# Layer 0's input projections: one 512-column product of the weights' high part with both parts of the input, in turns of 256 features

## The chip, the cores and the metric

The kernel runs on one core of a Trainium2 chip, as one launch. The metric is the time of the whole launch on the device, in microseconds. The times shown are the median of three runs; the profile comes from one more execution with the hardware profiler on.

## The reference

Two layers of a decoder trunk over 256 tokens of width 2048, in float32. Layer 0 is the one that the change touches:

```python
h = rms_norm(x, g_pre)
u = h @ w_in                      # (256 x 2048) @ (2048 x 8192)
xr, zr, xm, zm = jnp.split(u, [2048, 4096, 6144], axis=-1)
xr = causal_dwconv(xr, ...);  yr = rg_lru(xr, ...)
xmc = silu(causal_dwconv(xm, ...)); q, k = block_diag(xmc, ...); v = block_diag(xm, m_wv)
ym = head_norm(mlstm_chunkwise(q, k, v, ig, fg)) + m_skip * xmc
y = concat([yr * silu(zr), ym * silu(zm)])
x = x + rms_norm(y @ w_out, g_post)
```

Layer 1 is an RWKV-7 mixer with an input projection of 2048 x 16384 and an output projection of 4096 x 2048, with the same pre-norm, post-norm and residual.

## The kernel before, in words

**Number format.** The large products keep more precision than one pass of TensorE in fp32r gives. Each operand is split into a high part (a cast to fp32r) and a low part (the rest). A product is then the sum of three: weights high with input high, weights high with input low, weights low with input high. In the trace the parts of the weights are `whi` and `wlo`, the parts of the input `hh` and `hl`, those of the mixers' output `yh` and `yl`.

**Input projections.** `in_proj` (L242) makes 512 features of all 256 tokens. It takes eight weight tiles of 128 partitions x 1024 floats (two slabs of 128 input rows, 512 features each, 512 KB, one request of SyncE each in `load_w`, L216). `split_w` (L202) casts a tile on ScalarE (`whi`) and subtracts on VectorE (`wlo`). `in_mms` (L221) then issues 24 products: the weights are the stationary block (128 x 128), the input (features on partitions, 256 tokens) moves. Two PSUM banks (`gb`) hold the four blocks of 128 features. Layer 0 has 16 such projections, in three groups: four for `xm` (L680), four pairs for the LRU branch and its gate (L689), four for the mLSTM gate (L709). Layer 1 has 32 of the same form. There are four buffers for raw weights, three for `whi`, three for `wlo`.

**Output projections.** `out_proj` (L261) turns the roles round: the mixers' output is the stationary block, 512 columns of weights move, 768 products of 512 columns in each layer.

**The input.** `to_features` (L334) normalises the input and turns it so that features lie on partitions: a product with a diagonal matrix (`dg`), out of PSUM through ScalarE (`hh`) and VectorE (`hl`, L361 to L366). The first slab of 512 features is made ahead, the other three are made within the first projection, one when `in_proj` finds that it is needed soon (`next(grow[0])`).

**Order.** The order on TensorE is written out: `InOrder` (L102) chains its instructions. `Weave` interleaves the side work of the mixers (generators such as `mlstm_in`, `head`, `lru`) with the projections: `wv_.tick(dt)` moves a planned clock on, and each generator tells by `yield` when its next piece is due; `wv_.drain` issues what is left of one. The splits have a higher priority than other work of ScalarE and VectorE, and `Behind` (L123) keeps later rows behind them; the rest is ordered by the scheduler. Each engine runs its rows in that order. Because helpers issue everything, the trace shows all of TensorE's products at L117 or L120 and all of ScalarE's and VectorE's rows at L133; the names of the tiles tell them apart. `mb` are the PSUM banks of the side work.

**What takes a projection's result.** For `xm`, two ScalarE copies bring it to SBUF (`xm`), and `mlstm_in` of that block runs beside the next projection; its 80 products stand as one block behind that projection (`wv_.drain(prev)`). For the LRU branch, the convolution reads PSUM (`conv`, output `yc`); for the gates, `silu2` does.

Of the kernel before, what the change touches and what calls it, by code (L numbers as in the profile page):

```python
# [7 lines left out]
F32 = mybir.dt.float32  # L8
F32R = mybir.dt.float32r
# [4 lines left out]
P = 128  # L14
# [130 lines left out]
def two_layers(ctx, tc, x, gpost, cst, selc, v0, v1, w_in0, w_out0, w_in1, w_out1, lruw, qkvw,  # L145
# [9 lines left out]
    hp = ctx.enter_context(tc.tile_pool(name="hp", bufs=8))  # L155
# [3 lines left out]
    pg = ctx.enter_context(tc.tile_pool(name="pg", bufs=4, space=PS))  # L159
# [3 lines left out]
    def gbank():  # L163
        return pg.tile([P, 512], F32, name="gb", tag="gb")
# [56 lines left out]
    def in_mms(banks, hi, lo, pc, h, nft, tick):  # L221

        def mm(part, kk, f, hx, first=False, last=False):
            pe.matmul(banks[f // 2][:, (f % 2) * T:(f % 2 + 1) * T], lhsT=part[:, kk, f * P:(f + 1) * P], rhs=hx,
                      start=first, stop=last, skip_group_check=True)

        hs = [tuple(t[:, (2 * pc + kk) % 4, :] for t in h[(2 * pc + kk) // 4]) for kk in range(2)]
# [14 lines left out]
    def in_proj(wsrc, h):  # L242

        banks = [gbank(), gbank()]
# [7 lines left out]
    def half(banks, f):  # L252
        return banks[f // 2][:, (f % 2) * T:(f % 2 + 1) * T]

    def split_y(src, yl):
        yh = hp.tile([P, 4, T], F32R, name="yh", tag="hp")
# [4 lines left out]
    def out_proj(wsrc, get_y, evac, tick, finish, after, room=None):  # L261
# [22 lines left out]
        pair = [[gbank(), gbank()] for _ in range(2)]  # L284
# [9 lines left out]
        for c in range(2, 4):  # L294
            banks = [gbank(), gbank()]
# [38 lines left out]
    def to_features(xs, dg, g, warm):  # L334
# [14 lines left out]
        def tiles():  # L349
            banks[2] = [gbank(), gbank()]  # L350
# [5 lines left out]
            for c in range(4):  # L356
# [35 lines left out]
    def silu2(banks, sz):  # L392

        for b in range(2):
            bk = banks[b].rearrange("p (a t) -> p a t", a=2)
# [24 lines left out]
    with ExitStack() as l0:  # L420
# [257 lines left out]

        prev = None
# [9 lines left out]
        for c in range(4):  # L689
            lw = t4("lw")  # L690
            nc.sync.dma_start(lw.rearrange("p a t -> p (a t)"), lruw[:, c, :])
            banks = in_proj(w_in0[c * 8:(c + 1) * 8], h)
# [9 lines left out]
            banks = in_proj(w_in0[(4 + c) * 8:(5 + c) * 8], h)  # L702
# [6 lines left out]
        for c in range(4):  # L709
            banks = in_proj(w_in0[(12 + c) * 8:(13 + c) * 8], h)  # L710
# [31 lines left out]
    with ExitStack() as l1:  # L742
# [39 lines left out]
        def loras():  # L782

            banks = [gbank(), gbank()]
# [374 lines left out]
        for g in range(NG):  # L1159
            st = sts[g]  # L1160
            banks = in_proj(w_in1[(8 + g) * 8:(9 + g) * 8], h)
# [10 lines left out]
            banks = in_proj(w_in1[g * 8:(g + 1) * 8], h)  # L1172
# [4 lines left out]
            banks = in_proj(w_in1[(24 + g) * 8:(25 + g) * 8], h)  # L1177
# [7 lines left out]
            banks = in_proj(w_in1[(16 + g) * 8:(17 + g) * 8], h)  # L1185
# [116 lines left out]
```

## Time and profile before

| What | Value |
|---|---|
| Median of 3 runs | 1917.0 us (1916.63 to 1918.4) |
| The profiled execution's own time | 1918.1 us |
| Its span, first to last instruction | 1916.3 us |
| Granted TensorE clock, mean | 0.995 |
| TensorE busy | 1890.5 us, 16506 instructions |
| TensorE weight loads | 1753.2 us, 16507 instructions |
| VectorE busy | 1394.7 us |
| ScalarE busy | 1045.2 us |
| Transfers | 299.63 MB, mean 156 GB/s |
| Packets of the request queue | 86768, 45.0% of 16 engines' time |

A row of the chain or of the timeline gives the start in us from the span's start, the duration in us, the engine, and how many instructions were merged (x192). A group's row gives the line, the engine, the operation, output and inputs with their shapes, the count, busy time in us and the mean duration of one in ns; the durations of products overlap, so a pace is read from the chain and not from the mean. A row of the windows gives a stretch, its length, the busy time of TensorE, its weight loads, VectorE, ScalarE and GpSimd with instruction counts, the granted clock, the transfers' busy share and GB/s.

### The profile page before, as it was taken

To read this page: it belongs to the slowest core of one execution; us is meant where nothing else is said; L and a number is where in the kernel's file an instruction comes from. 1 tells how busy PE (TensorE), PEld (TensorE's weight loads), DVE (VectorE), ACT (ScalarE), POOL (GpSimd) and SP (SyncE) were. 2 spreads that over 40 slices of the span, in tenths; PEclk is the share of its full clock that TensorE was granted. 3 is DMA by queue.
4 is the path that set the end of the run, shared out by engine and by line. 5 is a ranking of instruction groups with operands and counts; after the bars stand their busy time and mean duration, and the time that the engine had idled before them with its cause. 6 is when DMAs were issued, how large, how long until landed. Compare 5 with 4: busy or idle time off the path is not lost.

```text
span 1916.3 us, 39538 instructions
## 1 busy us (share of the span) xinstructions
PE 1890.5 (99%) x16506; PEld 1753.2 (91%) x16507; DVE 1394.7 (73%) x2302; ACT 1045.2 (55%) x1609; POOL 59.1 (3%) x84
## 2 busy tenths in 40 slices
PE   9999999999999999999999999999999999999998
PEld 8999999999888899989999999999999999997886
DVE  5667777767555679879689689597796896895544
ACT  6445666645444546555565555655655655555442
POOL 0000000000000000000000000000000000000000
PEclk9999999999999999999999999999999999999999
DMA  7333544445666444423434334344343433356654
GB/s 254 138 133 111 176 165 171 152 173 197 214 202 202 165 144 147 155 106 137 143 130 143 123 130 157 109 150 146 116 147 133 141 133 133 122 186 201 211 202 156
DMA packets 86947, 299.63 MB, mean 156 GB/s; under 512 B 9576, under 2 KB 12392, under 8 KB 86768
## 3 DMA queue, kind: packets, MB, share of 16 engines
q1 hardware_dynamic: 86768, 297.11, 45.0%
q8 instruction: 129, 2.11, 0.4%
q14 instruction: 50, 0.41, 0.1%
HBM read 289.20 MB, written 7.86 MB: 155 GB/s over the span
## 4 chain that ended last, share of the span: by engine, by line
PE 93%; DVE 4%; ACT 1%; issue 1%; DMA 1%; POOL 0%; SPq 0%; DVEq 0%; POOLq 0%; ACTq 0%
PE gb L117 75%; PE mb L117 17%; DVE wlo L133 2%; PE mb L120 1%; ACT whi L133 1%; DVE wb L133 1%; DMA raw<-in_w_in_dram 0%; DVE rt L133 0%; DVE Tb L133 0%; DMA xq<-in_x_dram 0%; DVE tf L133 0%; DVE Ab L133 0%; DVE yT L133 0%; ACT ZT L133 0%; ACT vt L133 0%
## 5 line engine op out<-in xcount | busy, mean ns | idle before, releaser
L133 DVE TENSOR_TENSOR wlo<-raw,whi 128x1024 fp32r<-128x1024 f32 x509 | 619.6, 1218 | 344.2 <-ACT whi L133 308.4
L133 ACT CAST whi<-raw 128x1024 fp32r<-128x1024 f32 x509 | 532.3, 1048 | 553.4 <-PE gb L117 505.1
L117 PE MATMUL gb<-hh,whi 128*128 128x256 f32 x3120 | 793.5, 290 | 2.9 <-ACT whi L133 2.9
L117 PE MATMUL gb<-hl,whi 128*128 128x256 f32 x3120 | 773.7, 284 | 0.5 <-DVE hl L133 0.5
L117 PEld LDWEIGHTS gb<-hh,whi 128*128 128x128 f32 x3120 | 598.8, 192 | 13.6 <-ACT whi L133 3.7
L117 PEld LDWEIGHTS gb<-hl,whi 128*128 128x128 f32 x3120 | 600.0, 192 | 1.9 <-DVE hl L133 1.1
L117 PE MATMUL gb<-hh,wlo 128*128 128x256 f32 x3120 | 454.0, 286 | 0.0
L117 PEld LDWEIGHTS gb<-hh,wlo 128*128 128x128 f32 x3120 | 405.5, 192 | 4.2 <-issue 0.7
L117 PE MATMUL gb<-whi,yl 128*128 128x512 f32 x500 | 136.9, 392 | 0.5 <-DVE yl L133 0.5
L117 PE MATMUL gb<-whi,yh 128*128 128x512 f32 x500 | 136.5, 392 | 0.0
L117 PE MATMUL gb<-wlo,yh 128*128 128x512 f32 x500 | 135.7, 390 | 0.0
L117 PEld LDWEIGHTS gb<-whi,yl 128*128 128x128 f32 x500 | 93.2, 188 | 20.4 <-DVE yl L133 0.9
L117 PEld LDWEIGHTS gb<-wlo,yh 128*128 128x128 f32 x500 | 93.5, 188 | 19.7
L117 PEld LDWEIGHTS gb<-whi,yh 128*128 128x128 f32 x500 | 93.0, 188 | 19.3
L133 DVE TENSOR_TENSOR Tb<-Tb,tf 64x31 f32<-64x31 f32 (+15 forms) x248 | 82.5, 333 | 6.1
L133 DVE TENSOR_TENSOR tf<-Ab,Tb 64x31 f32<-64x31 f32 (+15 forms) x248 | 81.8, 330 | 4.5
L117 PE MATMUL mb<-AR,BK 64*128 64x128 f32 (+1 forms) x1024 | 58.0, 253 | 7.0 <-DVE AR L133 6.0
L117 PEld LDWEIGHTS mb<-AR,BK 64*128 64x128 f32 (+1 forms) x1024 | 50.2, 161 | 13.3 <-PE gb L117 7.1
L133 DVE TENSOR_TENSOR UV<-mb,Gn 64x256 f32<-64x256 f32 x64 | 26.9, 421 | 34.6 <-PE mb L117 33.4
L133 ACT ACTIVATE zz<-kP,dv 128x256 f32<-128x256 f32 x64 | 32.3, 505 | 22.9 <-DVE kP L133 12.4
L117 PEld LDWEIGHTS mb<-UV,At 128*64 128x64 f32 (+1 forms) x1024 | 35.0, 137 | 10.3 <-issue 2.2
L1140 POOL TENSOR_TENSOR vr<-vr,mhalf 128x8 f32<-128x8 f32 x16 | 28.3, 1771 | 505.5 <-DVE vr L133 505.5
(259 smaller groups left out, 1859.7 us busy)
## 6 DMA issues: line engine op xcount, KB each, us to landing
raw<-in_w_in_dram SPq DMA_DIRECT2D x384, 512.0 KB, 3.2
raw<-in_w_out_dram SPq DMA_DIRECT2D x128, 512.0 KB, 4.2
y1d<-zt SPq DMA_DIRECT2D x7, 512.0 KB, 3.5
yraw<-y1d SPq DMA_DIRECT2D x7, 512.0 KB, 3.8
l<-in_lora_dram SPq DMA_DIRECT2D x8, 384.0 KB, 4.3
xq<-in_x_dram SPq DMA_DIRECT2D x8, 256.0 KB, 4.4
lw<-in_lruw_dram SPq DMA_DIRECT2D x4, 512.0 KB, 4.9
xr<-in_x_dram SPq DMA_DIRECT2D x8, 256.0 KB, 6.3
```

Of the source, the lines that this page charges most:

```text
L117: return self._chain(self.eng.matmul(*a, **k))
L120: return self._chain(self.eng.transpose(**k))
L133: r = op(*a, **k)
L1140: pool.tensor_tensor(vr, vr, mhalf[:, 0:8], ALU.pow)
```

## The change

Layer 0's `in_proj` is rewritten; layer 1 keeps the old one under the name `in_proj1`. The high and low part of the input now lie beside each other in one tile `hx` (per slab row: 256 tokens of the high part, then 256 of the low), so that one product of 512 columns multiplies the weights' high part with both. A PSUM bank then holds one block of 128 features: the left half collects high with high, the right half high weights with the low input and low weights with the high input (products of 256 columns). As two banks hold only 256 features that way, a projection is done in two turns of 256 features, each over all 2048 input rows. A weight tile has 512 input rows of 256 features and comes by two requests with pieces of 256 floats. At a turn's end ScalarE copies the right half to an SBUF tile `u`, and VectorE adds the left half to it; what follows reads `u` instead of PSUM. The pools change to match: `hp` has four tiles of double size (`split_y` fills one in two steps), `pg` two pairs of banks. The planned clock moves on by 4 x 0.42 + 2 x 0.44 us for a tile of 16 products, where it was 6 x 0.44 for 24.

```diff
-    hp = ctx.enter_context(tc.tile_pool(name="hp", bufs=8))
+    hp = ctx.enter_context(tc.tile_pool(name="hp", bufs=4))
...
-    pg = ctx.enter_context(tc.tile_pool(name="pg", bufs=4, space=PS))
+    pg = ctx.enter_context(tc.tile_pool(name="pg", bufs=2, space=PS))
...
+    def gpair():
+        return pg.tile([P, 2, 512], F32, name="gb", tag="gb")
...
+    def in_proj(wsrc, h, mk):
+        u = None
+        for j in range(2):
+            t = gpair()
+            for pc in range(4):
+                raw = wp.tile([P, 2, 512], F32, name="raw", tag="raw", bufs=RAW_BUFS)
+                for n in range(2):
+                    src = wsrc[2 * pc + n].rearrange("p (k f) -> p k f", k=2)[:, :, j * 256:(j + 1) * 256]
+                    nc.sync.dma_start(raw[:, n].rearrange("p (k f) -> p k f", k=2), src)
+                hi, lo = (w.rearrange("p n (k f) -> p (n k) f", k=2) for w in split_w(raw))
+                if len(h) < 4 and len(h) <= pc + 1:
+                    next(grow[0])
+                for kk in range(4):
+                    for f in range(2):
+                        pe.matmul(t[:, f, :], lhsT=hi[:, kk, f * P:(f + 1) * P], rhs=h[pc][:, kk].rearrange("p a t -> p (a t)"),
+                                  start=(pc == 0 and kk == 0), stop=False, skip_group_check=True)
+                    wv_.tick(0.42)
+                for kk in range(4):
+                    for f in range(2):
+                        pe.matmul(t[:, f, T:2 * T], lhsT=lo[:, kk, f * P:(f + 1) * P], rhs=h[pc][:, kk, 0, :],
+                                  start=False, stop=(pc == 3 and kk == 3), skip_group_check=True)
+                    if kk % 2:
+                        wv_.tick(0.44)
+            if u is None:
+                u = mk()
+            act.copy(u[:, 2 * j:2 * j + 2, :], t[:, :, T:2 * T])
+            dve.tensor_tensor(u[:, 2 * j:2 * j + 2, :], t[:, :, 0:T], u[:, 2 * j:2 * j + 2, :], ADD)
+        return u
...
     def split_y(src, yl):
-        yh = hp.tile([P, 4, T], F32R, name="yh", tag="hp")
+        if not yhs:
+            pair = hp.tile([P, 2, 4, T], F32R, name="yh", tag="hp")
+            yhs.extend([pair[:, 1], pair[:, 0]])
+        yh = yhs.pop()
...
-                hh = hp.tile([P, 4, T], F32R, name="hh", tag="hp")
-                hl = hp.tile([P, 4, T], F32R, name="hl", tag="hp")
+                hx = hp.tile([P, 4, 2, T], F32R, name="hx", tag="hp")
                 for i in range(4):
                     bf = half(banks[c], i)
-                    activ(hh[:, i, :], bf, AF.Copy, scale=g(4 * c + i))
-                    dve.scalar_tensor_tensor(hl[:, i, :], bf, g(4 * c + i), hh[:, i, :].bitcast(F32), MUL, SUB)
-                h.append((hh, hl))
+                    activ(hx[:, i, 0, :], bf, AF.Copy, scale=g(4 * c + i))
+                    dve.scalar_tensor_tensor(hx[:, i, 1, :], bf, g(4 * c + i), hx[:, i, 0, :].bitcast(F32), MUL, SUB)
+                h.append(hx)
...
-            banks = in_proj(w_in0[(8 + c) * 8:(9 + c) * 8], h)
+            xm = in_proj(w_in0[(8 + c) * 8:(9 + c) * 8], h, u0)
             wv_.drain(prev)
-            xm = t4("xm")
-            for b in range(2):
-                act.copy(xm[:, 2 * b:2 * b + 2, :], banks[b].rearrange("p (a t) -> p a t", a=2))
             prev = wv_.add(mlstm_in(c, xm))
```

Three places show what moves. The first is TensorE at the start of layer 0's first projection; `dg` with `xq` are the turns of the input into feature order, four of a bank in a row. Before:

```order
L117 MATMUL mb<-dg,xq 128x128 x8
L117 MATMUL gb<-dg,xq 128x128 x4
L117 MATMUL mb<-dg,xq 128x128 x8
L117 MATMUL gb<-hh,whi 128x256
L117 MATMUL gb<-hl,whi 128x256
...
L117 MATMUL gb<-hh,wlo 128x256 x8
```

Now:

```order
L117 MATMUL gb<-hx,whi 128x512 x8
L117 MATMUL gb<-hx,wlo 128x256 x8
L117 MATMUL gb<-dg,xq 128x128 x4
L117 MATMUL gb<-hx,whi 128x512 x8
L117 MATMUL gb<-hx,wlo 128x256 x8
L117 MATMUL mb<-dg,xq 128x128 x8
L117 MATMUL gb<-hx,whi 128x512 x8
```

A weight tile has 16 products instead of 24, and the next turn of the input stands behind each of the first two tiles. In all, TensorE has 1024 products fewer; from the first output projection on its rows are the same as before.

The second place is VectorE at the same time, where the pieces of the input's slabs (`hx`, out of `gb` for the third slab) and the splits (`wlo`) share the engine. Now, from the second weight tile on:

```order
L133 SCALAR_TENSOR_TENSOR hx<-mb,vec_97,hx 128x256
L133 TENSOR_SCALAR lt<-vec_97 128x16
L133 TENSOR_TENSOR wlo<-raw,whi 128x1024
L133 SCALAR_TENSOR_TENSOR hx<-gb,vec_97,hx 128x256
L133 TENSOR_TENSOR wlo<-raw,whi 128x1024
L133 SCALAR_TENSOR_TENSOR hx<-gb,vec_97,hx 128x256
L133 TENSOR_TENSOR wlo<-raw,whi 128x1024
L133 SCALAR_TENSOR_TENSOR hx<-gb,vec_97,hx 128x256
L133 TENSOR_TENSOR lt<-vec_97,lt 128x16
L133 SCALAR_TENSOR_TENSOR hx<-mb,vec_97,hx 128x256
L133 TENSOR_SCALAR lt<-lt 128x16
L133 SCALAR_TENSOR_TENSOR hx<-mb,vec_97,hx 128x256
```

The row behind these is the third slab's last piece (`hx` out of `gb` again). Before, the rows of the constants' table (`lt`) and more splits stood between the slabs' pieces, which were spread over twice as many weight tiles.

The third place is VectorE at the end of the second `xm` projection, around the blocks of the mLSTM weights (`we`). Before:

```order
L133 SCALAR_TENSOR_TENSOR xm_792<-th,xc 128x1024
L133 TENSOR_TENSOR we<-qkvs,cs_112 128x128 x3
L133 TENSOR_TENSOR wlo<-raw,whi 128x1024
L133 TENSOR_TENSOR we<-qkvs,cs_112 128x128 x9
L133 TENSOR_TENSOR wlo<-raw,whi 128x1024
L133 TENSOR_TENSOR we<-qkvs,cs_112 128x128 x3
```

Now:

```order
L133 SCALAR_TENSOR_TENSOR xm_682<-th,xc 128x1024
L133 TENSOR_TENSOR we<-qkvs,cs_112 128x128 x3
L133 TENSOR_TENSOR wlo<-raw,whi 128x1024
L133 TENSOR_TENSOR we<-qkvs,cs_112 128x128 x8
L133 TENSOR_TENSOR wlo<-raw,whi 128x1024
L133 TENSOR_TENSOR u<-gb,u 128x512
L133 TENSOR_TENSOR we<-qkvs,cs_112 128x128 x4
```

The addition of the projection's second turn, which waits for its last product, stands ahead of the last four `we` blocks. In layer 1, VectorE and ScalarE keep their instructions, but some of them stand in another order than before.

More of the change, by code (lines that the diff above doesn't have):

```diff
@@ L158, in two_layers, with gbanks @@
     sp = ctx.enter_context(tc.tile_pool(name="small", bufs=2))
-    pg = ctx.enter_context(tc.tile_pool(name="pg", bufs=4, space=PS))
+    pg = ctx.enter_context(tc.tile_pool(name="pg", bufs=2, space=PS))
     pm = ctx.enter_context(tc.tile_pool(name="pm", bufs=4, space=PS))
     dr = ctx.enter_context(tc.tile_pool(name="dr", bufs=1, space=bass.MemoryType.DRAM))
-    def gbank():
-        return pg.tile([P, 512], F32, name="gb", tag="gb")
+    def gpair():
+        return pg.tile([P, 2, 512], F32, name="gb", tag="gb")
+    def gbanks():
+        b = gpair()
+        return [b[:, 0], b[:, 1]]
     def mbank():
@@ L225, in mm @@
                       start=first, stop=last, skip_group_check=True)
-        hs = [tuple(t[:, (2 * pc + kk) % 4, :] for t in h[(2 * pc + kk) // 4]) for kk in range(2)]
+        hs = [[h[(2 * pc + kk) // 4][:, (2 * pc + kk) % 4, part, :] for part in range(2)] for kk in range(2)]
         for kk in range(2):
@@ L240, in two_layers, with in_proj1 @@
     grow = [None]
-    def in_proj(wsrc, h):
-        banks = [gbank(), gbank()]
+    def in_proj(wsrc, h, mk):
[26 more added lines that the diff above has]
+        return u
+    def in_proj1(wsrc, h):
+        banks = gbanks()
         for pc in range(8):
@@ L252, in half @@
     def half(banks, f):
+        if not isinstance(banks, list):
+            return banks[:, f, :]
         return banks[f // 2][:, (f % 2) * T:(f % 2 + 1) * T]
+    yhs = []
     def split_y(src, yl):
-        yh = hp.tile([P, 4, T], F32R, name="yh", tag="hp")
+        if not yhs:
+            pair = hp.tile([P, 2, 4, T], F32R, name="yh", tag="hp")
+            yhs.extend([pair[:, 1], pair[:, 0]])
+        yh = yhs.pop()
         act.copy(yh, src)
@@ L282, in piece @@
                     wv_.tick(tick)
-        pair = [[gbank(), gbank()] for _ in range(2)]
+        pair = [gbanks() for _ in range(2)]
         for c in range(2):
@@ L294, in out_proj @@
         for c in range(2, 4):
-            banks = [gbank(), gbank()]
+            banks = gbanks()
             spare = room() if c == 3 and room else []
@@ L349, in tiles @@
         def tiles():
-            banks[2] = [gbank(), gbank()]
+            banks[2] = gbanks()
             keep_warm(warm[0], banks[2][0])
@@ L394, in silu2 @@
         for b in range(2):
-            bk = banks[b].rearrange("p (a t) -> p a t", a=2)
+            bk = banks[b].rearrange("p (a t) -> p a t", a=2) if isinstance(banks, list) else banks[:, 2 * b:2 * b + 2, :]
             s = sz[:, 2 * b:2 * b + 2, :]
@@ L691, in two_layers @@
             nc.sync.dma_start(lw.rearrange("p a t -> p (a t)"), lruw[:, c, :])
-            banks = in_proj(w_in0[c * 8:(c + 1) * 8], h)
+            banks = in_proj(w_in0[c * 8:(c + 1) * 8], h, u0)
             if c == 0:
@@ L701, in two_layers @@
             heads.append([wv_.add(head(hd)) for hd in (2 * c, 2 * c + 1)][1])
-            banks = in_proj(w_in0[(4 + c) * 8:(5 + c) * 8], h)
+            banks = in_proj(w_in0[(4 + c) * 8:(5 + c) * 8], h, u0)
             wv_.drain(g1_)
@@ L709, in two_layers @@
         for c in range(4):
-            banks = in_proj(w_in0[(12 + c) * 8:(13 + c) * 8], h)
+            banks = in_proj(w_in0[(12 + c) * 8:(13 + c) * 8], h, u0)
             wv_.drain(heads[c])
@@ L782, in loras @@
         def loras():
-            banks = [gbank(), gbank()]
+            banks = gbanks()
             for pc in range(8):
@@ L1160, in two_layers @@
             st = sts[g]
-            banks = in_proj(w_in1[(8 + g) * 8:(9 + g) * 8], h)
+            banks = in_proj1(w_in1[(8 + g) * 8:(9 + g) * 8], h)
             if g:
@@ L1171, in two_layers @@
             st["inv"] = wv_.add(inverse(g, st))
-            banks = in_proj(w_in1[g * 8:(g + 1) * 8], h)
+            banks = in_proj1(w_in1[g * 8:(g + 1) * 8], h)
             wv_.drain(st["keys"])
@@ L1176, in two_layers @@
             st["scores"] = wv_.add(scores(g, st), 1)
-            banks = in_proj(w_in1[(24 + g) * 8:(25 + g) * 8], h)
+            banks = in_proj1(w_in1[(24 + g) * 8:(25 + g) * 8], h)
             if g:
@@ L1184, in two_layers @@
                 sts[g + 1]["decay"] = wv_.add(decay(g + 1, sts[g + 1]), 3)
-            banks = in_proj(w_in1[(16 + g) * 8:(17 + g) * 8], h)
+            banks = in_proj1(w_in1[(16 + g) * 8:(17 + g) * 8], h)
             st["v"] = gt("vt", "vt")
```

1 line of the change is left out of this document (added).

## The prediction

> **What bounds the kernel now.** I read the page's busy times and its chain of waits first, to see which engine sets the end.
>
> ```profile
> PE 1890.5 (99%) x16506; PEld 1753.2 (91%) x16507; DVE 1394.7 (73%) x2302; ACT 1045.2 (55%) x1609; POOL 59.1 (3%) x84
> PE 93%; DVE 4%; ACT 1%; issue 1%; DMA 1%; POOL 0%; SPq 0%; DVEq 0%; POOLq 0%; ACTq 0%
> ```
>
> TensorE is busy nearly throughout, and 93% of the chain that ended last is its products. Busy does not mean at its peak, so the next view is the chain in order of time, in layer 0, which the change touches: start, duration, and how many instructions ran without a wait.
>
> ```profile
> 29.96 34.56 PE gb L117 x288
> 64.52 11.65 PE mb L117 x80
> 76.17 23.02 PE gb L117 x192
> 99.19 11.76 PE mb L117 x80
> 110.95 23.04 PE gb L117 x192
> ...
> 468.35 174.61 PE gb L117 x768
> ```
>
> One input projection is 8 weight loads of 24 products, 192 products of 256 columns. The chain goes through 192 of them in 23.02 to 23.04 us without naming any other engine: 23.03 / 192 = 119.95 ns each. The last row is layer 0's output projection, 768 products of 512 columns: 174.61 / 768 = 227.36 ns each. Both rows hold every product of their stretch, so nothing missing from the trace distorts the two paces. Two products of 256 columns take 239.90 ns and one of 512 takes 227.36: 12.54 ns are paid per instruction and not per column. From the same two rows, a column costs (227.36 - 119.95) / 256 = 0.4196 ns and an instruction 119.95 - 107.41 = 12.54 ns. That is what the change can remove. In layer 0 nothing but TensorE's own pace sets the time from 30 to 468 us, so what is saved there comes off the end, unless a wait replaces it.
>
> **The products.** A projection becomes 64 products of 512 columns (high weights on both parts of the input) and 64 of 256 (low weights on the high part). The columns are the same 49,152; 64 instructions and 64 weight loads fall away. Time: 64 x 227.36 + 64 x 119.95 = 14.55 + 7.68 = 22.23 us against 23.03, 0.80 us less. Sixteen projections: **-12.8 us**. In the output projection the 512 columns are weights and the stationary block is activations, here it is the other way round; type, sizes and one weight load per product are the same, so I take its pace whole.
>
> The Trainium skill speaks against this: "TensorE: Matmul & The Clock Gate", section "Back-to-back issue gap", gives an isolated gap of N / 2.4 + 2.5 ns, so two products of 256 would cost only 2.5 ns more than one of 512, an estimate of 2.6 us for the 1,024 pairs. The trace's 119.95 and 227.36 ns do not agree with that page's 109 and 216, and the measured pair decides the sum.
>
> **The turns' ends.** There are 32 turns of 256 features. Each ends with a ScalarE copy of 128x512 out of PSUM and a VectorE addition of the same size. Prices from the nearest rows: an `xm` copy, and a VectorE operation with one operand in PSUM.
>
> ```profile
> 102.31 0.58 ACT L133 COPY xm<-gb 128x512 f32<-128x512 f32 x1
> L133 DVE TENSOR_TENSOR og<-gb,gp 128x512 f32<-128x512 f32 x16 | 10.4, 682 | 0.0
> ```
>
> A projection gets 1.2 us more of ScalarE (nothing more in the four `xm` projections, whose copies go) and 1.36 us more of VectorE. What hides it is the slack of these engines, read from the windows (length, PE, PEld, DVE, ACT busy, clock, DMA share, GB/s) and from VectorE's own waits:
>
> ```profile
> 111.00:134.00 23.00, 23.00 (x193) 23.00 (x192) 14.66 (x26) 10.72 (x12) 0.00 (x0) 1.00 0.42 144
> 180.00:214.00 34.00, 34.00 (x273) 33.43 (x273) 29.34 (x39) 23.86 (x35) 0.11 (x1) 1.00 0.40 141
> 116.87 1.23 DVE L133 TENSOR_TENSOR wlo<-raw,whi 128x1024 fp32r<-128x1024 f32 x1 [1.66 <-ACT whi L133]
> 119.75 1.23 DVE L133 TENSOR_TENSOR wlo<-raw,whi 128x1024 fp32r<-128x1024 f32 x1 [1.66 <-ACT whi L133]
> 104.27 0.98 PE L117 MATMUL mb<-wif,we 128*128 128x40 f32 x8
> ```
>
> In the mLSTM projections VectorE is busy 14.66 of 23 us and waits 1.66 us at a time for the next cast. The tightest stretch is 180 to 214, where it has 4.7 us free; three additions take 2.0 of them. The one new wait with something behind it is the addition of a projection's second turn: VectorE stands until the last product and the copy are through (0.58 us), adds (0.68), and only then makes the last four `we` blocks that the mLSTM products need. Four of them come to about 0.9 us, and a split of 1.23 us can stand ahead: ready some 3.4 us after the projection's end. TensorE first uses such a block (with `wif`) 104.27 - 99.19 = 5.1 us after it, so this wait is covered by 1.7 us. ScalarE's next casts wait behind the copy, but they run two loads ahead. If the cover of the tight stretch is gone, up to 2 us are lost; if all holds, 0. I take **+0.5**.
>
> **The first projection.** A turn walks over all of the input, so the four slabs of it that are normalised on the way are needed in 11 us instead of 23. Timeline and chain at the start:
>
> ```profile
> 5.75 6.89 DMA raw<-in_w_in_dram
> 13.74 1.23 DVE L133 TENSOR_TENSOR wlo<-raw,whi 128x1024 fp32r<-128x1024 f32 x1 [0.88 <-ACT whi L133]
> 14.88 2.83 DVE L133 SCALAR_TENSOR_TENSOR hl<-mb,vec,hh 128x256 fp32r<-128x256 f32 x7
> 15.41 0.39 PE L117 MATMUL gb<-hl,whi 128*128 128x256 f32 x1 [0.33 <-DVE hl L133]
> 17.86 1.22 DVE L133 TENSOR_TENSOR wlo<-raw,whi 128x1024 fp32r<-128x1024 f32 x1
> 18.99 0.47 DVE L133 SCALAR_TENSOR_TENSOR hl<-mb,vec,hh 128x256 fp32r<-128x256 f32 x1
> 21.37 1.05 PE L117 MATMUL gb<-dg,xq 128*128 128x128 f32 x8
> 28.18 1.78 PE mb L117 x16
> ```
>
> TensorE starts at 15.41 as before. A load's 16 products take 22.23 / 8 = 2.78 us; with the two turns into feature order (1.05 and 1.78 us) the third load starts at 15.41 + 2.78 + 1.05 + 2.78 + 1.78 = 23.80, and its fourth row of weights, reached after six products (1.36 us), needs the third slab's last piece at 25.16. VectorE starts its next work at 19.39 (18.99 plus 0.40, the pace of the seven pieces in 2.83 us) and by its new order does three splits (17.86 to 18.99, so 1.14 each), six slab pieces (0.40 each) and two short table rows (0.1 each) before that piece is there: 6.0 us, 25.4. Counted by full durations instead it is 26.2. Stall 0.2 to 1.1; if ScalarE's casts hold it up as well, 2; below nothing it cannot be. I take **+0.7**. The fourth slab comes 1.2 to 2 us later, while the third load still runs, so it costs nothing.
>
> **The weights' transfers.** A tile of 512 KB came in one request of 4 KB pieces; now it comes in two, in pieces of 1 KB. The lora weights (pieces of 768 bytes, 192 KB a request) show what small pieces cost.
>
> ```profile
> 664.00:680.00 16.00, 16.00 (x137) 16.00 (x136) 10.80 (x28) 7.09 (x11) 1.07 (x2) 1.00 0.23 62
> 660.18 23.75 SPq L787 DMA_DIRECT2D raw<-in_lora_dram  x8
> 10.31 5.01 SPq L218 DMA_DIRECT2D raw<-in_w_in_dram  x4
> raw<-in_w_in_dram SPq DMA_DIRECT2D x384, 512.0 KB, 3.2
> ```
>
> 4 KB pieces: 144 GB/s at a share of 0.42, so 343 GB/s with all engines busy, 1.53 us a tile. Pieces of 768 bytes: 62 / 0.23 = 270 GB/s, 1.94 us. Pieces of 1 KB lie between; TensorE uses a tile in 2.78 us. Four buffers allow a tile three loads, 8.3 us, from request to use, against 3.2 us of landing. So it is hidden in the steady state. At the start it is not: the chain waits for the first tile from 5.75 to 12.64 us, and ScalarE casts it before anything else. Its second half stands ahead of the same small tables as before. Bounds 0 to 0.4 us (1.94 - 1.53), 1 if SP's queue, which let four requests through in 5.01 us there, holds the second half back: **+0.3**.
>
> **Layer 1** has the same TensorE order, but some VectorE and ScalarE rows swap places, and these engines end waits there.
>
> ```profile
> PE gb L117 75%; PE mb L117 17%; DVE wlo L133 2%; PE mb L120 1%; ACT whi L133 1%; DVE wb L133 1%; DMA raw<-in_w_in_dram 0%; DVE rt L133 0%; DVE Tb L133 0%; DMA xq<-in_x_dram 0%; DVE tf L133 0%; DVE Ab L133 0%; DVE yT L133 0%; ACT ZT L133 0%; ACT vt L133 0%
> ```
>
> The splits are 2% of the chain, some 38 us. A tenth of it either way would be near 3 us: **0, from -3 to +3**. The larger `hp` and `pg` buffers change nothing: each is freed by the same last reader as the two it replaces.
>
> **Sum.** -12.8 + 0.5 + 0.7 + 0.3 + 0 = -11.3. The profiled execution took 1918.1 us (span 1916.3 and 1.8 around it) and would take 1906.8. The median of the runs, 1917.0, is 1.1 lower, so **1905.7**. All terms at their low ends: 1917.0 - 12.8 - 3 = 1901; all at their high ends: 1917.0 - 12.8 + 2 + 2 + 1 + 3 = 1912.
>
> **Rivals.**
> 1. *The gain is half eaten.* VectorE is in order, and each of the 32 additions now waits for a product. If those stops delay a split by 0.16 us each, 5 us go. For it: 86% busy from 180 to 214. Against it: splits run two loads ahead, and the chain names no VectorE work between 30 and 468 us. 1905.7 + 5 = 1911.
> 2. *No gain.* A product of 512 columns with weights as the stationary block costs nearly two of 256, because the 12.54 ns belong to the output projection's operands. With 2.5 ns left of it per pair: 1917.0 - 2.6 + 1.5 = 1916. Against it: the rows differ in nothing else that the trace shows. This time is the one that the Trainium skill's "TensorE: Matmul & The Clock Gate" would give by the rule above.
> 3. *Slower: transfers become the bound.* Requests double and pieces quadruple. It decides when a tile of 1 KB pieces takes longer than 2.78 us plus the gain's share, 11.3 / 128 = 0.09, so from 2.87 us. At 3.0 us a tile: 128 x 0.22 = 28 - 11 = 17 more, 1934. For it: at the start SP passed four requests in 5.01 us, 1.25 each, so eight in turn would need 10 us for four tiles, 2.5 each, not far from 2.87. Against it: 1.94 us a tile by the lora rows.
>
> **Chances.** The forecast 0.66, own range 1901 to 1912; half eaten 0.16; no gain 0.10; slower 0.08. A measurement of this kernel tells about 0.2% (3.8 us) from no change, so the first two count as faster (0.82), the third as the same, the fourth as slower. The range 1901 to 1913 holds the first two and leaves out 0.18.
>
> **What would show it.** In the chain, 128 products of a projection in 22.2 us, and the output projection starting near 457 instead of 468.35. If rival 2 holds, near 23.0; the mean of the new products of 512 columns, now to be compared with
>
> ```profile
> L117 PE MATMUL gb<-whi,yl 128*128 128x512 f32 x500 | 136.9, 392 | 0.5 <-DVE yl L133 0.5
> ```
>
> would then be above 392 ns. For rival 1, VectorE rows (`u` or `wlo`) enter the chain before 457; for rival 3, TensorE and ScalarE wait for `raw` transfers. TensorE should wait for a `hx` piece near 25 us, under 1.2 us. The stretch behind the output projection's start keeps its 1448 us within 3. I am wrong if that stretch moves by more, or if the projections do not reach 22.4 us.

## The result, and the profile after

The changed kernel takes 1947.1 us (median of 4 runs, 1943.97 to 1949.9) against 1916.8 us of the kernel before on the same chip: a ratio of 1.0159, 95% interval 1.0145 to 1.0174. It is 30 us slower, where 1905.7 us and a gain of 11 were forecast. The profiled execution took 1943.97 us, with a span of 1942.2.

The busy line of its page:

```profile
PE 1892.5 (97%) x15483; PEld 1705.3 (88%) x15483; DVE 1417.6 (73%) x2334; ACT 1058.1 (54%) x1633; POOL 56.1 (3%) x84
```

TensorE has about 1,020 fewer instructions and is busy as long as before (1892.5 against 1890.5 us). What the missing products saved was used up elsewhere, so the chain in order of time comes next (start, duration, instructions):

```profile
76.47 22.36 PE gb L117 x128
...
110.48 22.36 PE gb L117 x128
...
311.06 0.60 DVE u L133
...
461.50 0.60 DVE u L133
...
465.69 0.56 DVE yn L133
466.25 0.14 issue
466.39 1.26 PE mb L120 x4
467.65 12.56 PE gb L117 x47
```

A projection is 128 products in 22.36 us, 0.67 less than the 23.03 of before. That part came. But output projection 0 starts at 467.65, only 0.70 earlier than before, and from there to the end it takes 1942.2 - 467.65 = 1474.6 us, where before took 1916.3 - 468.35 = 1447.9. So most of the gain is lost again within layer 0, and **26.6 us are lost in layer 1**, where TensorE's order of products is the same as before. (The profiled execution of the kernel before, 1918.1 us, is above its median, and that of the changed kernel is its fastest; so the spans differ by 26 us and the medians by 30.) What TensorE waits for, in the changed kernel (total us, times, longest):

```profile
PE mb L117 <- ACT sq L133: 10.2, 8, 1.4
PE mb L120 <- DVE yn L133: 7.2, 3, 5.0
PE mb L117 <- DVE AR L133: 6.6, 6, 1.1
PE gb L117 <- DVE og L133: 3.1, 2, 1.6
PE mb L117 <- issue: 3.1, 1, 3.1
...
PE gb L117 <- DVE hx L133: 1.3, 3, 0.7
```

The same view of the kernel before:

```profile
PE mb L117 <- DVE AR L133: 6.0, 6, 1.0
...
PE mb L117 <- ACT sq L133: 1.0, 2, 0.8
...
PE gb L117 <- DVE hl L133: 0.5, 2, 0.3
```

`yn` belongs to layer 0: it is a mixer head's normalised output, which TensorE transposes. `sq`, `AR` and `og` belong to the stretch behind output projection 0. `sq` are the squares of layer 1's keys: ScalarE and VectorE bring the projection of the keys out of PSUM, shifted in time (`kt`), ScalarE squares them, and 16 small products (128x2) sum them. One such place, in the timeline of the kernel before (start, duration, engine):

```profile
958.25 0.84 ACT L133 ACTIVATE kt<-gb,dv 128x256 f32<-128x256 f32 x2
...
958.76 0.87 DVE L133 SCALAR_TENSOR_TENSOR kt<-gb,vec,kt 128x255 f32<-128x255 f32 x2
...
959.27 0.47 ACT L133 ACTIVATE kt<-gb,dv 128x256 f32<-128x256 f32 x1 [0.18 <-DVE kt L133]
...
960.05 0.47 ACT L133 ACTIVATE kt<-gb,dv 128x256 f32<-128x256 f32 x1
...
961.83 0.90 ACT L133 ACTIVATE sq<-kt,vec 128x256 f32<-128x256 f32 x2
...
962.44 1.84 PE L117 MATMUL mb<-cs,sq 128*128 128x2 f32 x16
```

And the same place in the timeline of the changed kernel:

```profile
969.36 0.47 ACT L133 ACTIVATE kt<-gb,dv 128x256 f32<-128x256 f32 x1
...
969.87 0.48 DVE L133 SCALAR_TENSOR_TENSOR kt<-gb,vec,kt 128x255 f32<-128x255 f32 x1
...
970.39 0.47 ACT L133 ACTIVATE kt<-gb,dv 128x256 f32<-128x256 f32 x1 [0.55 <-DVE kt L133]
...
971.98 1.05 ACT L133 CAST whi<-raw 128x1024 fp32r<-128x1024 f32 x1
...
972.93 0.47 ACT L133 ACTIVATE kt<-gb,dv 128x256 f32<-128x256 f32 x1
...
973.55 1.40 PE L117 MATMUL mb<-cs,sq 128*128 128x2 f32 x12
...
973.81 1.22 DVE L133 TENSOR_TENSOR wlo<-raw,whi 128x1024 fp32r<-128x1024 f32 x1 [0.71 <-ACT sq L133]
...
974.95 0.48 DVE L133 SCALAR_TENSOR_TENSOR kt<-gb,vec,kt 128x255 f32<-128x255 f32 x1
...
975.79 0.49 ACT L133 ACTIVATE sq<-kt,vec 128x256 f32<-128x256 f32 x1
...
976.33 0.75 PE L117 MATMUL mb<-cs,sq 128*128 128x2 f32 x4 [1.38 <-ACT sq L133]
```

Before, ScalarE reads two pieces of the keys one right behind the other (958.25 to 959.09), VectorE's first read (958.76) begins while the second of them runs, and all four of ScalarE's reads are through 2.3 us after the first began (958.25 to 960.52). In the changed kernel it reads one, waits for VectorE's read, reads the next; the fourth read falls behind a cast and ends at 973.40, 4.0 us after the first began, VectorE's fourth stands behind a `wlo` split (973.81), and the last square starts 6.4 us after the first read (969.36 to 975.79), where it was about 4.0 (958.25 to about 962.2, the second of the two `sq` in their row). TensorE waits 1.38 us. The clock falls right behind it; windows of the changed kernel there (length, busy times, clock, DMA share, GB/s):

```profile
970.80:977.60 6.80, 5.42 (x63) 5.06 (x60) 5.72 (x12) 5.85 (x15) 0.00 (x0) 0.93 0.46 146
977.60:984.40 6.80, 6.80 (x56) 6.12 (x56) 3.94 (x11) 2.83 (x6) 1.65 (x1) 0.57 0.03 11
```

and of the kernel before behind its squares:

```profile
964.80:971.60 6.80, 6.76 (x85) 6.22 (x84) 6.62 (x15) 4.34 (x9) 1.80 (x1) 1.00 0.23 81
```

From 973.55 to 976.95, 3.4 us, TensorE ran nothing but 16 tiny products and the wait, and the next 6.8 us ran at a granted clock of 0.57. Before, the 16 take 1.84 us and the clock stays at 1.00. The Trainium skill, "TensorE: Matmul & The Clock Gate", section "What's actually happening", says that the clock is at half after an idle window of about 3.4 us, and that this window is free-running; the trace agrees in the length, though the 3.4 us here were not idle throughout. Summed over windows of 3.4 us, (1 - clock) x 3.4 us from 470 to 1762 us comes to 8.5 us before and 17.8 after.

So layer 1 nearly adds up: TensorE's waits from 470 us to the end, the groups of that view summed, rose from 14.0 to 29.6 us (15.6 more, 9.2 of them for `sq`, 3.1 for `og` and 3.1 for one start of the loras' second products, for which the profile names no releaser), the lower clock costs 9.3 more, and another 1.2 between 467.65 and 470 us, where the clock is 0.50: 26.1 of 26.6 us.

Why are the readers in turn? The waits in the built program, ScalarE's four reads of the keys of one group, before and after:

```
L133 ACTIVATE kt<-gb 128x256 [waits PE] x2
L133 ACTIVATE kt<-gb 128x256 [waits DVE]
L133 ACTIVATE kt<-gb 128x256 [waits DVE]

L133 ACTIVATE kt<-gb 128x256 [waits PE]
L133 ACTIVATE kt<-gb 128x256 [waits DVE]
L133 ACTIVATE kt<-gb 128x256 [waits DVE]
L133 ACTIVATE kt<-gb 128x256 [waits DVE]
```

Reads of one PSUM tile by two engines are put in a row, also across its two banks. The Trainium skill, "PSUM — Partial Sum Buffer", section "PSUM bank collisions raise a hardware error", gives a reason for it: two engines may not touch the same bank at once, reads included, so software adds a dependency. The traces show the dependency (0.55 us of waiting in the row at 970.39); no run here shows the two engines on one bank at once. By that reason it is needed bank by bank, as in the kernel before. The change made one tile of two banks (`gbanks`), and so one row of eight reads out of two rows of four that ran beside each other.

### The profile page after: what moved, and what is told of

Same layout as the page of the kernel before. It is cut to its first block, busy times and chain, and to the rows that moved or that the text cites. A ratio compares the mean times of both kernels' runs of the same rounds, so it can differ in the third digit from the quotient of the medians.

```text
span 1942.2 us, 37901 instructions
## 1 busy us (share of the span) xinstructions
PE 1892.5 (97%) x15483; PEld 1705.3 (88%) x15483; DVE 1417.6 (73%) x2334; ACT 1058.1 (54%) x1633; POOL 56.1 (3%) x84
## 4 chain that ended last, share of the span: by engine, by line
PE 85%; DVE 10%; ACT 3%; issue 1%; DMA 1%; POOL 0%; SPq 0%; DVEq 0%; POOLq 0%; ACTq 0%
PE gb L117 69%; PE mb L117 15%; DVE wlo L133 3%; DVE Ab L133 1%; ACT whi L133 1%; PE mb L120 1%; DVE tf L133 1%; DVE Tb L133 1%; DVE wb L133 1%; DVE rt L133 1%; ACT Yn L133 0%; DVE At L133 0%; DVE yT L133 0%; ACT sq L133 0%; DVE AR L133 0%
## 5 line engine op out<-in xcount | busy, mean ns | idle before, releaser
L117 PE MATMUL gb<-hx,whi 128*128 128x256 f32 (+1 forms) x5216 | 852.9, 311 | 4.3 <-ACT whi L133 2.9
L117 PEld LDWEIGHTS gb<-hx,whi 128*128 128x128 f32 x5216 | 721.0, 193 | 48.5 <-ACT whi L133 4.0
L117 PE MATMUL gb<-hx,wlo 128*128 128x256 f32 x3120 | 452.5, 286 | 0.0
L117 PEld LDWEIGHTS gb<-hx,wlo 128*128 128x128 f32 x3120 | 412.2, 191 | 13.9 <-issue 1.0
L117 PE MATMUL mb<-UV,At 128*64 128x64 f32 (+1 forms) x1024 | 43.8, 228 | 0.0
L133 DVE TENSOR_TENSOR At<-mb,cs 128x512 f32<-128x512 f32 x64 | 41.3, 675 | 0.0
```

Of the source, the lines that this page charges most:

```text
L117: return self._chain(self.eng.matmul(*a, **k))
L133: r = op(*a, **k)
```

## The experiments

All are compared with the kernel before on the same chip. "Start 0" is the start of output projection 0's first product in the timeline, where it overlaps the piece before it, so it stands 0.2 to 0.4 us ahead of the chain's row; "sq" is TensorE's wait for the squares over the run. Both are from the profiled execution.

| Run | Median us | Ratio (95% interval) | Start 0 | sq, us |
|---|---|---|---|---|
| kernel before | 1916.8 | 1 | 468.10 | 1.0 |
| changed kernel | 1947.1 | 1.0159 (1.0145 to 1.0174) | 467.30 | 10.2 |
| e1 pairs only | 1946.5 | 1.0167 (1.0150 to 1.0184) | 468.80 | 10.2 |
| e2 single banks in layer 1 | 1919.0 | 1.0014 (1.0005 to 1.0023) | 469.19 | 1.0 |
| e3 plan at 0.44 | 1917.7 | 1.0012 (1.0002 to 1.0021) | 467.25 | 1.0 |
| e4 pieces of 4 KB | 1921.3 | 1.0035 (1.0023 to 1.0047) | 470.29 | 1.0 |
| e5 shifts' readers in turn | 1934.8 | 1.0098 (1.0082 to 1.0115) | 468.44 | 9.3 |
| e6 order alone | 1928.2 | 1.0063 (1.0047 to 1.0079) | 468.56 | 8.5 |
| e7 first banks free | 1912.6 | 0.9983 (0.9972 to 0.9995) | 465.23 | 1.0 |
| e8 head plan | 1909.6 | 0.9964 (0.9952 to 0.9976) | 462.60 | 1.0 |
| e9 head first | 1907.6 | 0.9958 (0.9946 to 0.9971) | 458.54 | 1.0 |
| e10 all readers in turn | 1940.2 | 1.0125 (1.0109 to 1.0141) | 468.24 | 9.3 |
| e11 ScalarE's reads first | 1943.1 | 1.0142 (1.0128 to 1.0156) | 466.46 | 0.3 |
| e12 squares planned later | 1958.6 | 1.0219 (1.0200 to 1.0237) | 468.50 | 0.0 |
| e13 keys' readers in turn | 1940.1 | 1.0121 (1.0105 to 1.0137) | 468.50 | 9.3 |

### Which part of the change costs: e1 to e4

**e1** makes only the pairs, in the kernel before.

```diff
-    pg = ctx.enter_context(tc.tile_pool(name="pg", bufs=4, space=PS))
+    pg = ctx.enter_context(tc.tile_pool(name="pg", bufs=2, space=PS))
...
-        banks = [gbank(), gbank()]
+        banks = gbanks()
```

> The kernel before with one edit: the PSUM banks of the projections are taken as pairs in one tile (two tiles of two banks) instead of four single tiles; products, weights and input stay as before. Theory 1 (the pair tile makes layer 1 slower, because readers of one tile on ScalarE and VectorE wait for each other and the rows are ordered otherwise): 1917 + 27, between 1939 and 1948 us, with the stretch from the output projection of layer 0 to the end near 1474 us instead of 1448. Rival (layer 1's loss comes from what the new projection leaves behind: transfers, clock, a shifted plan): 1915 to 1920 us.

1946.5 us: the pairs alone cost what the whole change cost. Its waits behind output projection 0 are nearly those of the changed kernel:

```profile
PE mb L117 <- ACT sq L133: 10.2, 8, 1.4
PE mb L117 <- DVE AR L133: 6.6, 6, 1.1
PE mb L117 <- issue: 3.3, 1, 3.3
PE gb L117 <- DVE og L133: 3.1, 2, 1.6
```

**e2** is the changed kernel with four single banks from output projection 0 on.

```diff
+        pairs.close()
+        pgs.append(ctx.enter_context(tc.tile_pool(name="pg", bufs=4, space=PS)))
```

> The changed kernel, but from layer 0's output projection on the banks are four single tiles again; the pairs live only while layer 0's input projections run. Theory 1: the 27 us of layer 1 come back, 1916 to 1923 us, and VectorE's and ScalarE's rows there are those of before. Rival (transfers, clock, plan): 1942 to 1948, as the changed kernel.

1919.0 us: 28 of the 30 us come back. But the 10.7 us that sixteen projections save (16 x 0.67) are not there; TensorE still waits 7.2 us for `yn`.

**e3** is e2 with the planned clock moved on by 0.44 instead of 0.42 for a step of high products, 21.12 units a projection as before the change (20.48 in it).

```diff
-                    wv_.tick(0.42)
+                    wv_.tick(0.44)
```

> As the run before, and the planned clock moves on by 2.64 us a weight tile (0.44 instead of 0.42 after each row of 512-column products), as before the change. Theory 2 (with 2.56 us the last head's products are planned too late, so that TensorE waits for the head's normalisation right before the output projection, 5.0 us and a stretch at half clock): 6 to 9 us less than the run before, near 1911. Rival (the wait comes from VectorE having more to do, the additions, and only moves): within 2 us of the run before.

1.3 us less than e2, where 6 to 9 were expected; the intervals of the two overlap, so no gain is shown. It is the rival that came: the wait only moved.

```profile
PE mb L120 <- DVE yn L133: 4.5, 3, 3.2
...
PE gb L117 <- DVE u L133: 2.3, 1, 2.3
```

The wait for `u` comes from how e2 and e3 are made: a pool that is closed and opened again has to wait for the last addition (e7 goes round it).

**e4** is e3 with the weights laid out so that a tile comes in one request with pieces of 4 KB; every engine's rows are the same.

```diff
-                for n in range(2):
-                    src = wsrc[2 * pc + n].rearrange("p (k f) -> p k f", k=2)[:, :, j * 256:(j + 1) * 256]
-                    nc.sync.dma_start(raw[:, n].rearrange("p (k f) -> p k f", k=2), src)
+                raw = load_w(wsrc[4 * j + pc])
```

> As the run before, and the host lays layer 0's input weights out by turns, so that a weight tile is again one request of 512 KB in pieces of 4 KB; all rows of TensorE, VectorE and ScalarE are the same. If the small pieces are hidden, as the prediction had it: within 1 us of the run before. If they delay the first tile: 1 to 2 us less, with the first product near 15.4 instead of 17.3 us. If they slow TensorE's reads as well (22.36 us a projection instead of 22.23): 3 to 4 us less.

1921.3 us, 3.6 more than e3, and the first product (15.56 us) no earlier than in e3 (15.17). The expectation's 17.3 us is where the changed kernel's third product starts (17.27), not its first. None of its three cases came, and the small pieces and the doubled requests cost nothing that shows. Where e4 is slower, the traces tell: TensorE's waits sum to 25.5 us against e3's 25.4, but its clock is lower. The stretch at half clock behind the first wait for `yn` is longer (from 300 to 330 us the mean clock is 0.83, 0.94 in e3), and all six executions of e4 have a mean clock of 0.991 to 0.994, e3's ten 0.992 to 0.996. Why the same waits lower the clock more is open.

### What about the pairs costs: e5, e6, e10, e11, e13

**e5** keeps the kernel before with its single banks and chains the reads of the two banks in layer 1's three shifts.

```diff
-                activ(o[:, f, :], u, AF.Copy, scale=col(omu, i))
-                dve.scalar_tensor_tensor(...)
+                last = in_turn(last, act.activation(...))
+                last = in_turn(last, dve.scalar_tensor_tensor(...))
```

`in_turn` adds a dependency of each read on the read before it.

> The kernel before with its own four single banks and buffers; the only edit: in the shifts of layer 1 (three of the four projections of each group) each read of the two banks waits for the read before it, ScalarE and VectorE in turn over all eight, also from one bank to the other, as the pair tile made them. Theory (it is the chain of the readers that costs, not the size of what is released): most of the loss of the pairs, 1935 to 1946 us, with ScalarE's rt waiting for VectorE's rt some 28 us in all, and at least five more stretches of half clock than before. Rival 1 (a pair is released as one, and the next product waits for it): at most 1921 us, since every bank is still released alone here. Rival 2 (z's bank readers, the loras' copies and the tile transposes carry the loss): at most 1925 us, since those are as before here.

1934.8 us: 18.3 us more than before, by an edit that only chains readers. That is just under what the theory named, and above both rivals: every bank is still released alone here, and z, the loras and the turns into feature order are as before. ScalarE's `rt` waits 27.0 us for VectorE's, as the theory had it (9.6 before), and the sums used above nearly add up to the loss: TensorE's waits from 470 us on are 23.5 us (14.0 before), the lower clock costs 17.1 (8.5 before). TensorE's longest waits:

```profile
PE mb L117 <- ACT sq L133: 9.3, 8, 1.4
PE mb L117 <- DVE AR L133: 6.6, 6, 1.1
```

**e6** asks for the same order and adds no wait between engines (`NoSync` in place of `Sync`).

> As the run with the readers in turn, but only the order of the rows on ScalarE and VectorE is asked for, no wait between the engines is added by it; the scheduler then stands the rows otherwise than in either (188 of VectorE's 1668 rows of layer 1 and 67 of ScalarE's 1080 differ from the kernel before). If the waits cost: 1916 to 1924 us. If the changed places of the rows alone cost: 1935 us or more. Between the two: both.

1928.2 us, 11.6 us more than before: between the two. The scheduler places later rows by that order, and the wait for `sq` is 8.5 us even without the added waits: the fourth piece of the keys stands behind a cast on ScalarE (963.76, then the read at 964.71) and a split on VectorE (965.58, then 966.73). So most of that wait comes from where the chain puts the rows, and less from waiting as such. How the 18.3 us of e5 divide between the two is not exact, since the rows of e6 do not all stand where those of e5 do.

**e10** chains the readers wherever the change had made a pair (also z's activation, the loras' copies, the rows behind the output projections, the third part of the input).

> The kernel before with its single banks; every pair of banks that the change put into one tile has its reads chained, one behind the other on ScalarE and VectorE (the shifts, z's activation, the loras' copies, the squares and products behind the output projections, the split of the third part of h). 25 of VectorE's 1668 rows of layer 1 and 8 of ScalarE's 1080 then stand otherwise than with the pairs. Theory (the chain of the readers is the whole price of the pairs): 1942 to 1950 us, as with the pairs alone (1946.5). Rival (the release of two banks as one has a part in it): 1938 us or less.

1940.2 us, 24.7 of the 30 us (the kernel before took 1915.4 on that chip). It lies between theory and rival. What the last 5 to 6 us of the pairs come from is open. Where the pairs wait 3.1 us for `og` (e1), e10 has no such wait; that would be the release of two banks as one, but no run takes that part alone. The start without a named releaser among the loras' products is there in e10 (4.6 us), e1 (3.3) and the changed kernel (3.1), and not in e5, which leaves the loras' reads as they were.

**e11** keeps the pairs and writes ScalarE's four reads of a shift ahead of VectorE's four, so that the chain changes its engine once instead of seven times.

```diff
             for f in range(4):
                 activ(o[:, f, :], u, AF.Copy, scale=col(omu, i))
+            for f in range(4):
+                i = sec * 32 + 4 * g + f
+                u = half(banks, f)
                 dve.scalar_tensor_tensor(...)
```

> The changed kernel with its pair tiles everywhere; the only edit: in the shifts of layer 1 ScalarE's four reads of a pair are written ahead of VectorE's four, so that the chain of readers changes its engine once instead of seven times. Theory (it is the number of hand-overs between the engines): ScalarE's wait for VectorE's rt goes, and at least 18 us of the loss come back, 1910 to 1929 us. Rival 1 (four activations in a row, 2 us, now stand ahead of the weights' high parts on ScalarE and make them late): 1930 us or more. Rival 2 (the release of the pair as one): above 1940 us.

1943.1 us: that theory falls, though ScalarE's wait for `rt` is gone. The number of hand-overs is not the price. The time lies in the range of both rivals, so it does not choose between them; the waits show what is late:

```profile
PE mb L117 <- DVE AR L133: 17.0, 6, 2.8
...
PE mb L117 <- ACT UV L133: 5.6, 6, 0.9
```

The squares are now in time (0.3 us), but VectorE starts its part of the shift only when ScalarE has read all four (in one group ScalarE's four end at 968.50 and VectorE's begin at 968.53); `AR`, which VectorE makes after the shifts, is late instead (17.0 us, 6.0 before), and `UV`, which ScalarE copies, by 5.6. Neither rival shows as a wait that grew much: TensorE's wait for `whi` is 3.4 us (2.9 before), that for `og` 3.1 as in e1. What the two separate banks gave, by these rows, was that both engines could read beside each other.

**e13** chains the readers of the keys' shift alone, one of the three of e5.

```diff
-                last = in_turn(last, ...)
+                last = in_turn(last if sec == 1 else None, ...)
```

> The kernel before with its single banks; of the readers' chains only that of the keys' shift is asked for, one of the three shifts of a group that the run with the readers in turn chained. Theory (only the keys' shift stands on the path: the squares wait for it): TensorE waits 8 us or more for sq, and at least two thirds of the 18.3 us of that run are there, 1928 to 1936 us. Rival (the three shifts share the price, or VectorE's later rows carry it): 1924 us or less.

1940.1 us, 23 us more than before, which is above the theory's range, and 5 more than with all three. A chain on the keys' shift alone is enough for the price. Two sums cover the 5 us: TensorE's waits from 470 us on are 27.4 us against e5's 23.5 (`AR` 2.3 more, `ZT` 1.6 more), and the halved clock, summed as above, costs 20.5 us against 17.1. Why chaining the other two shifts as well makes these smaller is not settled. TensorE waits in e13:

```profile
PE mb L117 <- ACT sq L133: 9.3, 8, 1.4
PE mb L117 <- DVE AR L133: 8.9, 6, 1.5
```

**e12** is the changed kernel with the squares' products planned later.

```diff
-            yield 2.4
+            yield 3.9
```

> The changed kernel with its pair tiles; the only edit: in layer 1 the products of the squares (mb from sq) are planned 3.9 instead of 2.4 units behind the shift of the keys, so that more projection products stand ahead of them on TensorE. Theory (the loss in layer 1 is that the squares come 1.3 us too late in each of seven groups, and the half clock behind each such wait): TensorE's wait for sq falls from 10.2 us to under 3, five or more half clock stretches go, and the time is 1920 to 1930 us instead of 1947. Rival (the later products make the keys' chain late for the inverse and the scores, since 464 rows of TensorE move): other waits take their place, above 1937 us.

1958.6 us: slower still, as its rival said. The wait for `sq` is gone, and the chain behind it is late:

```profile
PE mb L117 <- DVE AR L133: 12.6, 6, 2.1
PE mb L120 <- DVE At L133: 8.5, 6, 1.4
...
PE mb L117 <- ACT ZT L133: 6.8, 7, 1.1
```

At this setting the plan does not win back the time lost between the keys' projection and the squares; the work behind the squares is late in their place. Other settings were not tried.

### Where layer 0's gain went: e7 to e9

**e7** is e3, and output projection 0 takes its first two banks from the small products' pool, so that it need not wait for `u`.

```diff
-        pair = [gbanks() for _ in range(2)]
+        pair = [first(), gbanks()]
```

> The run with the plan at 0.44 and single banks in layer 1; the only edit: output projection 0 takes its first two banks from the small products' four, so its first product need not wait for the last addition of the turns. Theory: its first product stands at 464.5 to 465.3 instead of 467.25, no wait for u before it, and the time falls by 2 to 3 us from 1917.7 to about 1915. Rival (the wait moves to the next thing that is late there, the last transposes or the first weights): first product after 466.5, time within 1 us of 1917.7.

1912.6 us; the first product stands at 465.23, as expected, 2.0 us earlier. The time fell by 5.0, more than the expected 2 to 3; the spans of the two profiled executions differ by 2.6 (1914.9 and 1912.3), so the rest may be the spread between executions. It is below the kernel before.

**e8** also gives a head's second stage (from the products with `vtok` to the transposes of `yn`) 10.9 planned units instead of 9.38, takes them from its first stage, and raises the priority of its VectorE rows and of the turns' ends.

```diff
-            yield 15.36
+            yield 13.8
...
-            yield 9.38
+            yield 10.9
...
+            with tc.high_priority(offset=200):
```

> As the run before, and in layer 0 the heads' second stage is given 10.9 instead of 9.38 units of planned time and its first 13.8 instead of 15.36, and its VectorE work and the additions of the turns stand ahead in the priorities by 200 places. Theory (the plan was made for the old pace, and the product's gain was lost where the normalised head came late): the waits of TensorE for yn (4.5 us in three places, and a half clock behind the longest) go, output projection 0 starts at 458 to 462, and the time is 1907 to 1912 us, below the kernel before. Rival (the LRU's chain or the head's first stage is late next): TensorE waits as long for Dt or yc instead, and the time is 1914 us or more.

1909.6 us, as expected; the start, 462.60, is just behind the expected 458 to 462. One head still made TensorE wait for `yn`, 1.7 us in two pieces from 372 to 374 us.

**e9** is e8 with an offset of 2000.

> The run with the new head plan; the only edit: the heads' VectorE work and the additions stand 2000 places ahead in the priorities instead of 200. In that run one stall was left: VectorE's scan of yc (2.28 us), two lower parts, sz and y stand within the second head's chain, TensorE waits 1.7 us for yn at 372 us and its clock is halved behind it. Theory: this wait goes too, output projection 0 starts at 458 to 460, and the time is 1904 to 1908 us. Rival (what stood ahead of the head is late in its place: yc or the lower parts): the time is 1909 us or more.

1907.6 us, ratio 0.9958 (0.9946 to 0.9971). Output projection 0 starts at 458.54, and TensorE's waits no longer name `yn` or `u`:

```profile
PE mb L117 <- DVE AR L133: 6.0, 6, 1.0
...
PE gb L117 <- DVE hx L133: 1.3, 3, 0.7
...
PE mb L117 <- ACT sq L133: 1.0, 2, 0.8
```

The end of layer 0 in its chain has TensorE from the last projection through the transposes into the output projection:

```profile
449.97 8.38 PE gb L117 x48
458.35 0.44 PE mb L120 x4
458.79 16.39 PE mb L117 x72
```

This version beats both kernels: 7.9 us under the kernel before (1915.4 on that chip), near the 11 us of the forecast, but with a plan and priorities that the forecast did not have. What these alone would give the kernel before was not run; its TensorE waits for no `yn`.

## Why the prediction was wrong

**The step that failed** is the one on layer 1: "The larger `hp` and `pg` buffers change nothing: each is freed by the same last reader as the two it replaces", and with it 0, from -3 to +3. It looked at who frees a buffer. It did not ask who waits for whom among the readers of one buffer. e1 puts the whole 30 us there, e5 and e10 show that the chain of readers makes 18 to 25 of them, e13 that a chain on the keys' shift alone is enough for 23, and e6 that the places which the chain gives to the rows do much of it (11.6 us without the added waits). The last 5 us of the pairs are open. The order of rows that this step noticed ("some VectorE and ScalarE rows swap places") was its first sign, and it was priced by a tenth of the splits (a tenth of 38 us is 3.8, not near 3) instead of by the chain that ends at `sq`. The sign that the prediction named for being wrong is the one that came: the stretch behind the output projection's start moved by 26.6 us, not 3. The named start near 457 us did not come either (467.65).

**The products: right, a little too high.** 22.36 us against 22.23 forecast, 10.7 us for sixteen against 12.8. The pace of 512 columns with weights as the stationary block works out at (22.36 - 64 x 0.11995) / 64 = 229.4 ns, not 227.36. Rival 2 falls. By the rule of the Trainium skill, "TensorE: Matmul & The Clock Gate", section "Back-to-back issue gap", a projection would have stayed near 22.9 us, an estimate; the measured 22.36 does not agree with it.

**The turns' ends: the cover did not hold.** The place that the prediction watched, the `we` blocks of the mLSTM products, made no wait. But twice an addition is in the chain, at 311.06 and 461.50 us (0.60 each), behind a split (`wlo`) and ahead of rows of a head's normalisation, whose `yn` TensorE then waits for. "Nothing but TensorE's own pace sets the time" in layer 0 was true only by a narrow margin: side work is due by planned units, a projection's plan was shortened from 21.12 to 20.48 units, and VectorE got work on top. The shorter plan alone is not the reason, since e3 takes it back without a clear gain. From the third projection to output projection 0 it took 467.65 - 76.47 = 391.2 us, 1.0 less than before (468.35 - 76.17 = 392.2), where fourteen projections save 9.4. `yn` alone took 7.2 back. Of rival 1 both the mechanism (VectorE late) and the sign it named (`u` and `wlo` in the chain before 457 us) came; the late work was not the splits but the heads. e7 to e9 bring the gain back by plan, by order and by the two banks that output projection 0 starts with.

**The first projection and the transfers.** TensorE waits 1.1 us for `hx` there and 0.3 for `hl` before (the other 0.2 us of each row above are in layer 1): +0.8, forecast +0.7. The number is luck in part: these waits stand at the first weight tile (0.67 us at 16.09 and 0.44 at 17.27), where the prediction had none, since each product now needs both parts of a piece. At the third tile, where it had one, no wait is listed; the chain names `hx` there up to 26.80 us, and the tile's eight products take 2.47 us, where those of the second tile took 2.09. The first product stands at 16.09 (14.72 before), but also at 14.91 and 15.17 in e2 and e3 with the same requests, so this is the spread of the start and not a price; e4 gives no gain to larger pieces, so the +0.3 for the transfers does not show. Rival 3 falls: TensorE never waits for `raw`, and ScalarE waits for layer 0's input weights once, 1.2 us for the first tile (0.9 before).

So one term was right in size but partly in another place, one does not show, one was a fifth too high, one cover was missed (some 8 us), and a term put at zero was 27 to 30 us.

## What to carry to other kernels

Two PSUM banks in one tile are not two tiles: in this program every reader on one engine waits for the reader before it on another, across both banks, and the scheduler stands the rows around them otherwise. Before merging buffers, list not only who frees them but who reads them beside each other, and follow that to the first product that needs the result. When TensorE's work is made shorter, plans and slack that were measured in its old pace have to be set again, or the gain turns into waits of TensorE at the next product that other engines feed.

## What was not expected of the hardware

A wait of 1.4 us among 16 products of 2 columns was followed by half the clock: 3.4 us in all without a large product, then 6.8 us at a granted clock of 0.57. In the changed kernel six groups have this wait of 1.38 to 1.39 us, and behind each of them the clock falls to 0.50 within 2 us. In the kernel before seven groups have the same 16 products without a wait (1.84 us), and the clock stays at 1.00 behind all seven. It is not a fixed rule: in e13 one of six such waits (1.38 us, up to 1375.09 us) has a clock of 1.00 behind it. In layer 1 the lower clock cost 9.3 us more than before, beside 15.6 us of waits.
